# Key blocks of a two-mixer decoder layer: second copies by DMA, and another bank for the eighth value tile

## The chip, the core and the metric

The kernel runs on one core of one Trainium2 chip. The metric is the device time of one execution in microseconds (us). TensorE (PE) multiplies into eight PSUM banks, VectorE (DVE), ScalarE (ACT) and GpSimd (POOL) work on vectors, and SyncE (SP) issues nearly all DMAs of this kernel.

## The reference, cut to what matters

One decoder layer over 1024 tokens of width 1024. A normalised and modulated input `h` is projected to queries, keys and values of two token mixers with two key heads each, to gates and to a merge. One mixer is a banded attention (window 128, `swa`); the other adds a compressed, a block-selected (`slc`) and a banded attention (window 512, `win`).

```python
h = rms_norm(x, g_pre[l]) * (1.0 + scale[:, None, :]) + shift[:, None, :]
proj = h @ w_in[l]
q_a, kv_c, kv_s, kv_w, g_nsa, z_a, q_b, kv_b, z_b, merge = jnp.split(proj, pts, axis=-1)
o_a = gts[0] * o_cmp + gts[1] * o_slc + gts[2] * o_win
o_b = banded_attention(qb, kv_heads(kb_, ...), kv_heads(vb_, ...), slopes_b, SWA_WINDOW, sinks=sinks[l])
y = (sigmoid(m_a) * y_a + sigmoid(m_b) * y_b) @ w_out[l]
x = x + gate[:, None, :] * rms_norm(y, g_post[l])
```

## The kernel before

**Numbers in two parts.** Every large product is three matmuls. A float32 operand is split into a high part in TensorE's rounded format and a low part that is the rest; high x high, low x high and high x low are added in one PSUM bank. A score needs two matmuls: the query tile holds the 64 high rows of a head on one half of the partitions and its 64 low rows on the other, and the key tile must therefore hold the same key rows on both halves. That is the second copy this case is about. `kh` is the high part of the keys, twice; `kl` the low part, twice.

**Key blocks.** `k_block` (L488) takes a bank with the projected keys of two key heads, 64 rows each, and for each head r: ACT copies the high part to half r of the partitions (L500), DVE subtracts for the low part (L508), DVE copies both to the other half (L510, L511). Where the tile is that of a banded mixer's second half of the tokens, it also holds the last 128 columns of the first half in front (L503, L504); a `slc` tile has 64 columns of compressed keys there (L506, L507). The second head's L500 waits for the first head's L508. There are six key blocks: `swa` in two halves, and `slc` with `win` in two halves for each of two groups, so 12 heads and 24 second copies, and 8 copies of a first block.

**Stages.** (1) A prologue to about 56 us forms the first half of `h` and, while it arrives, four value tiles in banks `s`, `s`, `s`, `pt` and the first key and query columns in `fb`: banks `pj`, `pj`, `pt`. (2) Two compression inputs are projected, the second half of `h` is formed, and the value tiles five to seven are multiplied together (72 matmuls, L210 to L212) in the three `s` banks, then tile eight alone (24 matmuls). `v_out` (L238) takes a value tile off its bank: a high part on ACT (L242), a low part on DVE (L243), the gate columns on DVE (L244). (3) Next the compression's second halves (L187 onwards), its MLP, and gate projections. (4) Four units, two of `swa` and two of the other mixer, from about 180 us to 680 us: scores (L770, L773), softmax, transposes (L841), split of the weights (L847 on ACT, L848 on DVE), weighted values (L849, L852) into the one `pv` bank, which ACT and DVE read at the task's end (L861, L862). Projections for later work fill TensorE between them (L900 to L905). (5) The two output projections and the merge.

**What sets the order.** PSUM banks come from four rings: three `s`, two `pt`, one `pv`, two `pj`. A bank is reused when the last reader of its earlier content is done. The code is scheduled by the Tile framework, which simulates a timeline and writes each engine's instructions in a fixed order; `chain` ties the order of some of them (tags `act`, `dve`, `kout`, `pj`, ...). Each engine then runs its own list in order and waits on semaphores. SP issues DMAs in its listed order too: a DMA whose input is not ready holds all that stand behind it. Weights come in halves of 256 KB (`wraw`, three buffers), are split by ACT or DVE and POOL into `wh` and `wl` (six buffers each). At the end of a task `zt` is loaded and `od` stored by SP; `ot` and `zt` have one buffer each.

Of the kernel before, what the change touches and what calls it, by code (L numbers as in the profile page):

```python
# [7 lines left out]
F32 = mybir.dt.float32  # L8
# [6 lines left out]
P = 128  # L15
D = 1024
S = 1024
HS = 512
# [50 lines left out]
def hybrid_kernel(tc, io, out):  # L69
    nc = tc.nc  # L70
# [9 lines left out]
    def bank(tag):  # L80
        return ps.tile([P, 512], F32, tag=tag, name=f"b_{tag}", bufs=BANKS[tag])
# [3 lines left out]
    def chain(tag, ins):  # L85

        if tag in last and last[tag].ins.engine == ins.ins.engine:
            tc.add_manual_dep(
                ins.ins, last[tag].ins.name,
                mybir.DependencyInfo(mybir.DependencyClass.NoSync, mybir.DependencyReason.DATA), reason=tag)  # L90
        last[tag] = ins
# [88 lines left out]
    def proj_half(w, half, get, between=None):  # L180
        t = get()
        for kc in range(KC):
            mid = between() if between and kc == 2 else None
            if mid:
                after(mid, ins)
            wh, wl = (x[:, kc % KH, :] for x in w[kc // KH])
            ins = nc.tensor.matmul(t, lhsT=wh, rhs=hh[kc][half], start=(kc == 0), stop=False)  # L187
            if mid:
                after(ins, mid)
            if kc == 0:  # L190
                chain("pj", ins)
                if hold[0] is not None:
                    after(ins, hold[0])
            nc.tensor.matmul(t, lhsT=wh, rhs=hl[kc][half], start=False, stop=False)  # L194
            nc.tensor.matmul(t, lhsT=wl, rhs=hh[kc][half], start=False, stop=(kc == KC - 1))  # L195
        return t
# [8 lines left out]
    def v_products(half, k, i, t, w):  # L205

        sl = slice(i * P, i * P + P)
        wh, wl = w
        return [
            lambda: nc.tensor.matmul(t[:, :408], lhsT=hh[k][half][:, sl], rhs=wh, start=(k == 0), stop=False),  # L210
            lambda: nc.tensor.matmul(t[:, :408], lhsT=hh[k][half][:, sl], rhs=wl, start=False, stop=False),
            lambda: nc.tensor.matmul(t[:, :408], lhsT=hl[k][half][:, sl], rhs=wh, start=False, stop=(k == KC - 1))]  # L212
# [8 lines left out]
    def in_turn(products, between=(), at=2):  # L221

        for n in range(3):
            if n == at:
                for f in between:
                    f()
            for fs in products:
                ins = fs[n]()
                if n == 0:
                    chain("kout", ins)  # L230

    def dve(ins):
        chain("dve", ins)
        return ins

    def act(ins):
        chain("act", ins)
        return ins  # L238

    def v_out(i, t):  # L240
        tv = t[:, :384].rearrange("p (h d) -> p h d", h=6)
        high = nc.scalar.copy(V[i][:, :, 0, :], tv)  # L242
        low = nc.vector.tensor_tensor(V[i][:, :, 1, :], tv, V[i][:, :, 0, :].bitcast(F32), ALU.subtract)  # L243
        rest = nc.vector.tensor_copy(gates[:, i].rearrange("p b g r -> p (b g r)"), t[:, 384:408])  # L244
        act(high)
        dve(low)
        dve(rest)
# [15 lines left out]
    with tc.tile_pool(name="pro", bufs=1, reuse_waits="tile") as pro:  # L263
# [61 lines left out]
        vb = [bank(b) for b in ("s", "s", "s", "pt")]  # L325
        fb = [bank(b) for b in ("pj", "pj", "pt")]
# [68 lines left out]
        for k in range(KC):  # L395
            nxt = loads(k + 1) if k + 1 < KC else None
            t = pro.tile([P, HS], F32, name="ht", tag="ht", bufs=3)
# [91 lines left out]
    def k_block(keys, half, w, t=None, act=lambda i: i, dve=lambda i: i):  # L489
        if t is None:  # L490
            t = proj_half(w, half, lambda: bank("pj"))
        for r in range(2):
            src = t[64 * r : 64 * r + 64, :]

            pre, tag, bufs = (P, "kts", 8) if keys[r][0] == "slc" or half else (0, "kt", 6)
            khp = kq.tile([P, pre + HS], F32R, name="kh", tag=tag, bufs=bufs)
            klp = kq.tile([P, pre + HS], F32R, name="kl", tag=tag, bufs=bufs)
            kh, kl = khp[:, pre:], klp[:, pre:]
            hi, lo = kh[64 * r : 64 * r + 64, :], kl[64 * r : 64 * r + 64, :]
            chain(tag, act(nc.scalar.copy(hi, src)))  # L500
            if pre and keys[r][0] != "slc":
                before = K[(keys[r], 0)]
                nc.vector.tensor_copy(khp[:, :P], before[0][:, HS - P :].bitcast(F32))  # L503
                nc.vector.tensor_copy(klp[:, :P], before[1][:, HS - P :].bitcast(F32))  # L504
            elif pre:
                nc.vector.tensor_copy(khp[:, pre - 64 : pre], kc2[:, 0, keys[r][1], :].bitcast(F32))  # L506
                nc.vector.tensor_copy(klp[:, pre - 64 : pre], kc2[:, 1, keys[r][1], :].bitcast(F32))  # L507
            dve(nc.vector.tensor_tensor(lo, src, hi.bitcast(F32), ALU.subtract))  # L508
            o0, o1 = 64 - 64 * r, 128 - 64 * r
            dve(nc.vector.tensor_copy(kh[o0:o1, :], hi.bitcast(F32)))  # L510
            dve(nc.vector.tensor_copy(kl[o0:o1, :], lo.bitcast(F32)))  # L511
            K[(keys[r], half)] = (khp, klp)

    def q_fills(mixer, g, half):
# [2 lines left out]
    def k_fills(mixer, g, half):  # L517
        if mixer == "B":
            return [lambda: k_block([("swa", 0), ("swa", 1)], half, load_block("KB"))]
        return [lambda: k_block([("slc", g), ("win", g)], half, load_block(f"KA{g}"))]  # L520
# [33 lines left out]
    vb = [bank("s") for _ in range(3)]  # L554
    for k in range(KC):
        in_turn([v_products(1, k, i, vb[i], vw_all[k]) for i in range(3)])
    v_out(4, vb[0])
    t = bank("s")
    for k in range(KC):
        in_turn([v_products(1, k, 3, t, vw_all[k])])  # L560
    k_block([("swa", 0), ("swa", 1)], 0, None, fb[0], act, dve)
    v_out(5, vb[1])
    v_out(6, vb[2])
    v_out(7, t)
# [691 lines left out]
```

## Time and profile before

| | |
|---|---|
| median of 3 runs | 908.1 us (908.0 to 910.78) |
| profiled execution: its time | 909.31 us |
| its span, first to last instruction | 907.5 us |
| granted TensorE clock | 0.998 |
| PE busy, weight loads busy | 894.1 us (99%), 755.8 us (83%) |
| DVE, ACT, POOL busy | 554.3, 505.3, 352.8 us |
| share of DMA engines on the SP queue | 32.9% |

A row of the timeline gives the start in us, the time that the merged instructions took, engine, line, operation, tiles (output<-inputs, numbers left out), shapes and how many; in brackets the idle time of the engine before it, with what ended it. Consecutive matmuls overlap: the time of one (0.39 us for 512 columns) is longer than the distance to the next start (0.23 us), so distances are taken from start to start.

### The profile page before, as it was taken

The page shows a single profiled execution, that of the slowest core. Times are in us where ns is not written, and L with a number is a line of the kernel's source. Part 1 is how long each engine was busy: PE and PEld are TensorE (multiplying, and loading weights), DVE is VectorE, ACT ScalarE, POOL GpSimd, SP SyncE. Part 2 cuts the span into 40 slices and gives each one's busy share as a digit, 9 for nine tenths or more (in the row PEclk, how much of TensorE's full clock was granted, in tenths as well). Part 3 has the DMA queues.
Part 4 walks back from the last instruction along what each step waited for, and adds up shares of the span by engine and source line. Part 5 has one row for each costly group of instructions (what it writes and reads, how often), then busy time and mean ns, then how long its engine had stood idle before and what let it go on. Part 6 is the DMA issues. An engine that isn't in the chain of part 4 may idle for free.

```text
span 907.5 us, 14317 instructions
## 1 busy us (share of the span) xinstructions
PE 894.1 (99%) x4568; PEld 755.8 (83%) x4568; DVE 554.3 (61%) x1546; ACT 505.3 (56%) x1151; POOL 352.8 (39%) x422
## 2 busy tenths in 40 slices
PE   9999999999999999999999999999999999999997
PEld 8889888888888878888888878888887888887885
DVE  5866864475577787675576687566464372677322
ACT  5476732476676767665656667565564564441111
POOL 0000411364675866443545566453442375200000
PEclk9999999999999999999999999999999999999999
DMA  8872442333233312111211211111202587334422
GB/s 313 299 262 69 140 159 85 117 94 105 83 105 101 98 51 69 59 44 64 70 47 60 70 55 63 59 47 60 81 30 77 204 259 228 104 113 184 137 95 88
DMA packets 63870, 100.84 MB, mean 111 GB/s; under 512 B 7473, under 2 KB 24241, under 8 KB 63794
## 3 DMA queue, kind: packets, MB, share of 16 engines
q1 hardware_dynamic: 62640, 98.69, 32.9%
q10 hardware_dynamic: 1154, 1.23, 0.4%
q8 instruction: 36, 0.59, 0.3%
q14 instruction: 40, 0.33, 0.1%
HBM read 79.97 MB, written 19.92 MB: 110 GB/s over the span
## 4 chain that ended last, share of the span: by engine, by line
PE 94%; DVE 3%; ACT 1%; issue 1%; DMA 0%; POOL 0%; DVEq 0%; POOLq 0%; ACTq 0%
PE b_pt L841 8%; PE b_pj L900 7%; PE b_pj L904 7%; PE b_pj L905 7%; PE b_pj L194 5%; PE b_pj L195 5%; PE b_pj L187 5%; PE b_s L773 4%; PE b_s L770 4%; PE b_pv L852 4%; PE b_pv L849 4%; PE b_s L1140 1%; PE b_s L1139 1%; PE b_s L1141 1%; PE b_pt L294 1%; PE b_s L210 1%
## 5 line engine op out<-in xcount | busy, mean ns | idle before, releaser
L164 POOL TENSOR_TENSOR wl<-wraw,wh 128x512 fp32r<-128x512 f32 x102 | 132.8, 1305 | 140.2 <-ACT wh L161 91.9
L848 DVE TENSOR_TENSOR pl<-b_pt,ph 128x512 fp32r<-128x512 f32 x162 | 110.3, 686 | 55.5 <-ACT ph L847 54.6
L847 ACT CAST ph<-b_pt 128x512 fp32r<-128x512 f32 x162 | 93.5, 584 | 63.5 <-PE b_pt L841 52.7
L900 PE MATMUL b_pj<-hh,wh 128*128 128x512 f32 x288 | 117.1, 410 | 0.0
L905 PE MATMUL b_pj<-hh,wl 128*128 128x512 f32 x288 | 113.8, 395 | 0.0
L904 PE MATMUL b_pj<-hl,wh 128*128 128x512 f32 x288 | 113.3, 395 | 0.0
L195 PE MATMUL b_pj<-hh,wl 128*128 128x512 f32 x240 | 94.6, 394 | 0.0
L187 PE MATMUL b_pj<-hh,wh 128*128 128x512 f32 x240 | 94.5, 394 | 0.0
L194 PE MATMUL b_pj<-hl,wh 128*128 128x512 f32 x240 | 94.2, 392 | 0.0
L804 POOL TENSOR_SCALAR ps<-ps,rr,gates 128x128 f32<-128x128 f32 (+7 forms) x64 | 52.5, 822 | 94.6 <-DVE rr L796 50.0
L770 PE MATMUL b_s<-kh,q 128*128 128x256 f32 (+6 forms) x272 | 85.8, 322 | 0.0
L792 ACT ACTIVATE ps<-ps,mins 128x256 f32<-128x256 f32 (+7 forms) x96 | 64.9, 678 | 36.6 <-DVE mins L780 32.3
L773 PE MATMUL b_s<-kl,q 128*128 128x256 f32 (+6 forms) x272 | 83.8, 316 | 0.0
L161 ACT CAST wh<-wraw 128x512 fp32r<-128x512 f32 x94 | 57.8, 617 | 39.2 <-PE b_pj L194 13.6
L792 ACT ACTIVATE pw<-pw,mins 128x256 f32<-128x256 f32 (+4 forms) x96 | 60.7, 634 | 23.9 <-DVE mins L780 23.6
L849 PE MATMUL b_pv<-ph,V 128*128 128x512 f32 x162 | 65.5, 404 | 3.5 <-DVE ot L862 3.5
L852 PE MATMUL b_pv<-pl,V 128*128 128x512 f32 x162 | 67.9, 419 | 0.3
L905 PEld LDWEIGHTS b_pj<-hh,wl 128*128 128x128 f32 x288 | 54.1, 188 | 10.8
L863 POOL TENSOR_TENSOR ot<-ot,zt 64x512 f32<-64x512 f32 x32 | 41.7, 1303 | 55.0 <-DVE ot L862 43.5
L904 PEld LDWEIGHTS b_pj<-hl,wh 128*128 128x128 f32 x288 | 54.3, 189 | 8.8
L900 PEld LDWEIGHTS b_pj<-hh,wh 128*128 128x128 f32 x288 | 53.8, 189 | 7.8
L804 POOL TENSOR_SCALAR pw<-pw,rr,gates 128x640 f32<-128x640 f32 (+4 forms) x64 | 47.2, 741 | 31.7 <-DVE rr L796 28.6
(298 smaller groups left out, 2138.8 us busy)
## 6 DMA issues: line engine op xcount, KB each, us to landing
wraw<-in_w_blk SPq DMA_DIRECT2D x90, 256.0 KB, 2.9
wa<-in_w_adaT SPq DMA_DIRECT2D x24, 512.0 KB, 5.6
w1raw<-in_w SPq DMA_DIRECT2D x16, 256.0 KB, 3.2
od<-ot SPq DMA_DIRECT2D x64, 64.0 KB, 2.1
sp_MA<-sp SPq DMA_DIRECT2D x16, 256.0 KB, 2.0
wraw<-in_w_o SPq DMA_DIRECT2D x16, 256.0 KB, 3.0
wraw<-in_w_out SPq DMA_DIRECT2D x16, 256.0 KB, 3.4
t<-od SPq DMA_DIRECT2D x16, 256.0 KB, 3.9
```

The costliest lines, as they stand in the source:

```text
L164: chain("wl", nc.gpsimd.tensor_tensor(wl, raw, wh.bitcast(F32), ALU.subtract))
L187: ins = nc.tensor.matmul(t, lhsT=wh, rhs=hh[kc][half], start=(kc == 0), stop=False)
L194: nc.tensor.matmul(t, lhsT=wh, rhs=hl[kc][half], start=False, stop=False)
L195: nc.tensor.matmul(t, lhsT=wl, rhs=hh[kc][half], start=False, stop=(kc == KC - 1))
L770: ins = nc.tensor.matmul(sp[:, :n_in], lhsT=q, rhs=rh, start=True, stop=False)
L773: nc.tensor.matmul(sp[:, :n_in], lhsT=q, rhs=rl, start=False, stop=True)
L792: nc.scalar.activation(rows[r][:, :off], rows[r][:, :off], AF.Exp, scale=-1.0, bias=last_min[:, r : r + 1], accum_out=sums[:, r : r + 1])
L848: nc.vector.tensor_tensor(pl, t, ph.bitcast(F32), ALU.subtract)
L852: nc.tensor.matmul(pv, lhsT=v, rhs=pl, start=False, stop=(last and n == len(todo) - 1))
L900: ins = nc.tensor.matmul(self.t, lhsT=wh, rhs=hh[kc][self.half], start=(kc == 0), stop=False)
L904: nc.tensor.matmul(self.t, lhsT=wh, rhs=hl[kc][self.half], start=False, stop=False)
L905: ins = nc.tensor.matmul(self.t, lhsT=wl, rhs=hh[kc][self.half], start=False, stop=(kc == KC - 1))
```

## The change

In `k_block` the two copies of a first block (L503, L504) and the two second copies of each head (L510, L511) are no longer DVE instructions; each is a DMA from SBUF to SBUF on SP's queue. The 64 columns of compressed keys stay on DVE. In stage 2 the first key block is written ahead of the eighth value tile and ahead of the fifth tile's `v_out`, and the eighth tile's bank comes from the `pj` ring instead of the `s` ring.

```diff
@@ -500,15 +500,15 @@
             chain(tag, act(nc.scalar.copy(hi, src)))
             if pre and keys[r][0] != "slc":
                 before = K[(keys[r], 0)]
-                nc.vector.tensor_copy(khp[:, :P], before[0][:, HS - P :].bitcast(F32))
-                nc.vector.tensor_copy(klp[:, :P], before[1][:, HS - P :].bitcast(F32))
+                nc.sync.dma_start(khp[:, :P].bitcast(F32), before[0][:, HS - P :].bitcast(F32))
+                nc.sync.dma_start(klp[:, :P].bitcast(F32), before[1][:, HS - P :].bitcast(F32))
             elif pre:
                 nc.vector.tensor_copy(khp[:, pre - 64 : pre], kc2[:, 0, keys[r][1], :].bitcast(F32))
                 nc.vector.tensor_copy(klp[:, pre - 64 : pre], kc2[:, 1, keys[r][1], :].bitcast(F32))
             dve(nc.vector.tensor_tensor(lo, src, hi.bitcast(F32), ALU.subtract))
             o0, o1 = 64 - 64 * r, 128 - 64 * r
-            dve(nc.vector.tensor_copy(kh[o0:o1, :], hi.bitcast(F32)))
-            dve(nc.vector.tensor_copy(kl[o0:o1, :], lo.bitcast(F32)))
+            nc.sync.dma_start(kh[o0:o1, :].bitcast(F32), hi.bitcast(F32))
+            nc.sync.dma_start(kl[o0:o1, :].bitcast(F32), lo.bitcast(F32))
             K[(keys[r], half)] = (khp, klp)
 
     def q_fills(mixer, g, half):
@@ -554,11 +554,11 @@
     vb = [bank("s") for _ in range(3)]
     for k in range(KC):
         in_turn([v_products(1, k, i, vb[i], vw_all[k]) for i in range(3)])
-    v_out(4, vb[0])
-    t = bank("s")
+    k_block([("swa", 0), ("swa", 1)], 0, None, fb[0], act, dve)
+    t = bank("pj")
     for k in range(KC):
         in_turn([v_products(1, k, 3, t, vw_all[k])])
-    k_block([("swa", 0), ("swa", 1)], 0, None, fb[0], act, dve)
+    v_out(4, vb[0])
     v_out(5, vb[1])
     v_out(6, vb[2])
     v_out(7, t)
```

The order of the built programs shows three places. First DVE where the second half of `h` ends (L306) and the fifth to eighth value tiles are taken off; `b_pj_160` is the first keys' bank, `b_s_764` the fifth tile's. Before:

```order
L306 TENSOR_TENSOR hl7_117<-xh_640,hh7_101 128x512
L243 TENSOR_TENSOR V4_133<-b_s_764,V4_133 128x6x64
L244 COPY gates_85<-b_s_764 128x24
L508 TENSOR_TENSOR kl_868<-b_pj_160,kh_867 64x512
L510 CAST kh_867<-kh_867 64x512
L511 CAST kl_868<-kl_868 64x512
L508 TENSOR_TENSOR kl_874<-b_pj_160,kh_873 64x512
L510 CAST kh_873<-kh_873 64x512
L511 CAST kl_874<-kl_874 64x512
L243 TENSOR_TENSOR V5_134<-b_s_765,V5_134 128x6x64
```

And now, to the eighth tile in `b_pj_851`:

```order
L306 TENSOR_TENSOR hl7_117<-xh_640,hh7_101 128x512
L508 TENSOR_TENSOR kl_840<-b_pj_160,kh_839 64x512
L508 TENSOR_TENSOR kl_846<-b_pj_160,kh_845 64x512
L243 TENSOR_TENSOR V4_133<-b_s_764,V4_133 128x6x64
L244 COPY gates_85<-b_s_764 128x24
L243 TENSOR_TENSOR V5_134<-b_s_765,V5_134 128x6x64
L244 COPY gates_85<-b_s_765 128x24
L243 TENSOR_TENSOR V6_135<-b_s_766,V6_135 128x6x64
L244 COPY gates_85<-b_s_766 128x24
L634 MEMSET kcf_1092 128x128
L649 MEMSET vcf_1224 128x128
L243 TENSOR_TENSOR V7_136<-b_pj_851,V7_136 128x6x64
```

Both key subtractions moved ahead of the value tiles, and their four copies are gone. On PE the list is the same there but for the bank: the eighth tile's 24 matmuls are followed at once by the compression's projection into `b_pj_915` (L187), as before. In the built program the eighth tile's first matmul now waits for the second key subtraction (before: for the fifth tile's L244), and that L187 waits for the eighth tile's L244 (before: for the second key subtraction).

The second place is DVE in the third unit (and, with the same rows, in the fourth), where the keys of the second half of the tokens are made while a task ends. Before:

```order
L820 TENSOR_TENSOR pl_3765<-b_pt_3761,ph_3764 128x256
L503 CAST kh_3876<-kh_2987 128x128
L848 TENSOR_TENSOR pl_3829<-b_pt_3823,ph_3828 128x512
L508 TENSOR_TENSOR kl_3869<-b_pj_3754,kh_3868 64x512
L510 CAST kh_3868<-kh_3868 64x512
L511 CAST kl_3869<-kl_3869 64x512
L504 CAST kl_3877<-kl_2988 128x128
L506 CAST kh_5279<-kc2_137 128x64
L508 TENSOR_TENSOR kl_3877<-b_pj_3754,kh_3876 64x512
L510 CAST kh_3876<-kh_3876 64x512
L862 TENSOR_TENSOR ot_3775<-b_pv_3621,ot_3775 64x512
L511 CAST kl_3877<-kl_3877 64x512
```

Now:

```order
L820 TENSOR_TENSOR pl_3765<-b_pt_3761,ph_3764 128x256
L848 TENSOR_TENSOR pl_3829<-b_pt_3823,ph_3828 128x512
L508 TENSOR_TENSOR kl_3869<-b_pj_3754,kh_3868 64x512
L508 TENSOR_TENSOR kl_3877<-b_pj_3754,kh_3876 64x512
L506 CAST kh_5279<-kc2_137 128x64
L862 TENSOR_TENSOR ot_3775<-b_pv_3621,ot_3775 64x512
```

Six copies have left the list ahead of and around L862, which frees the `pv` bank. The third place is SP at the same point; now:

```order
L151 DMA wraw_4174<-in_w_blk 128x512
L503 DMA kh_3876<-kh_2987 128x128
L510 DMA kh_3868<-kh_3868 64x512
L511 DMA kl_3869<-kl_3869 64x512
L504 DMA kl_3877<-kl_2988 128x128
L510 DMA kh_3876<-kh_3876 64x512
L511 DMA kl_3877<-kl_3877 64x512
L151 DMA wraw_4315<-in_w_blk 128x512
L866 DMA od0_118<-ot_3775 64x2x128
L866 DMA od1_119<-ot_3775 64x2x128
```

Before, `wraw_4315` followed `wraw_4174` at once; the six key DMAs stand between them, and the stores of the task (`od`) come after. On all engines together the list differs in many small ways from about 95 us to 400 us and in the fourth unit around the key block, since the scheduler placed its fill-in work anew.

## The prediction

> **What bounds the kernel now.** I read the page's busy times and chain first, then the list of what PE waited for, then the timeline at each of those waits.
>
> ```profile
> PE 894.1 (99%) x4568; PEld 755.8 (83%) x4568; DVE 554.3 (61%) x1546; ACT 505.3 (56%) x1151; POOL 352.8 (39%) x422
> PE 94%; DVE 3%; ACT 1%; issue 1%; DMA 0%; POOL 0%; DVEq 0%; POOLq 0%; ACTq 0%
> PE b_pv L849 <- DVE ot L862: 3.5, 2, 1.8
> PE b_pt L294 <- DVE eps L309: 1.0, 1, 1.0
> PE b_s L210 <- DVE gates L244: 1.0, 1, 1.0
> PE b_pt L841 <- DVE pl L848: 0.6, 2, 0.3
> PE b_pt L614 <- ACT w L610: 0.3, 1, 0.3
> ```
>
> PE is busy for 99% of the span and holds 94% of the chain. The change takes no matmul away, so it can win only PE's waits. The list is all of them: 6.4 us, 1.0 of it (L294) at the very start. The other 5.4 us are five stops at three places that the change touches, and one (L614) just behind. DVE's total (61%) does not matter; only where it is late does.
>
> **First place: the eighth value tile.** The rows run from the last three matmuls of tiles five to seven to the first of tile eight.
>
> ```profile
> 75.59 0.82 ACT L303 ACTIVATE xh<-xh,mod 128x512 f32<-128x512 f32 x1
> 76.44 0.69 DVE L306 TENSOR_TENSOR hl<-xh,hh 128x512 fp32r<-128x512 f32 x1 [0.86 <-ACT xh L303]
> 79.18 0.72 PE L212 MATMUL b_s<-wvh,hl 128*128 128x408 f32 x3
> 79.94 0.58 ACT L500 CAST kh<-b_pj 64x512 fp32r<-64x512 f32 x1
> 80.56 0.17 DVE L244 COPY gates<-b_s 128x24 f32<-128x24 f32 x1
> 80.64 0.67 DVE L508 TENSOR_TENSOR kl<-b_pj,kh 64x512 fp32r<-64x512 f32 x1
> 80.87 0.42 PE L210 MATMUL b_s<-wvh,hh 128*128 128x408 f32 x1 [0.97 <-DVE gates L244]
> ```
>
> Matmuls of 408 columns start 0.186 us apart (24 of them from 80.87 to 85.39 are 0.188 each), so without a wait tile eight would begin at 79.18 + 3 x 0.186 = 79.74. It began at 80.87: **1.13 us lost**, from start to start. Now it waits for the two key subtractions instead. Their bank has been full since the prologue, and both stand right behind the last L306, which ends at 77.13. ACT is free at 76.41: L500 to 76.99, L508 from 77.13 to 77.80, second L500 to 78.41, second L508 to about 79.1. With the 0.14 us between L244's end (80.73) and PE's start that is 79.25, ahead of 79.74. The stop goes.
>
> It comes back behind the tile, because the projection that follows (L187) now takes the bank that tile eight leaves:
>
> ```profile
> 85.21 0.34 PE L212 MATMUL b_s<-wvh,hl 128*128 128x408 f32 x1
> 85.39 0.40 PE L187 MATMUL b_pj<-hh,wh 128*128 128x512 f32 x1
> 85.59 0.34 ACTq L630 DMA_DIRECT2D w2k<-in_w2k  x1
> 85.97 0.48 ACT L242 CAST V<-b_s 128x384 fp32r<-128x384 f32 x1 [3.15 <-PE b_s L212]
> 86.96 0.17 DVE L244 COPY gates<-b_s 128x24 f32<-128x24 f32 x1
> ```
>
> From the tile's last matmul (85.21) to the end of its L244 (87.13) are 1.92 us: the matmul's end, a DMA issue on ACT's queue, the high part, the low part, the gates. With 0.14 for the semaphore, L187 can start 2.06 us after that matmul, where 0.18 would do: **a new wait of 1.88 us**. Everything here stands 1.13 earlier, so L187 starts at 85.39 - 1.13 + 1.88 = 86.14. The first place loses **0.75 us** net. Queued behind that L187 are the compression and its MLP, all of PE's list; the queries (L485, L486) follow the eighth tile on ACT and DVE and are 1.13 us earlier than before, so the scores that need them do not stop PE again. The L614 stop (0.3 us) may go, since ACT's gate work moves ahead of it; I count 0 and leave it to the range.
>
> **Second and third place: the keys of the second half, in both long units.** From top to bottom POOL, DVE, ACT and PE of the third unit.
>
> ```profile
> 331.75 1.29 POOL L164 TENSOR_TENSOR wl<-wraw,wh 128x512 fp32r<-128x512 f32 x1
> 331.44 1.68 DVE L503 CAST kh<-kh 128x128 fp32r<-128x128 f32 x1
> 333.05 0.68 DVE L848 TENSOR_TENSOR pl<-b_pt,ph 128x512 fp32r<-128x512 f32 x1
> 333.65 0.67 DVE L508 TENSOR_TENSOR kl<-b_pj,kh 64x512 fp32r<-64x512 f32 x1
> 335.12 0.23 DVE L504 CAST kl<-kl 128x128 fp32r<-128x128 f32 x1
> 336.66 0.68 DVE L862 TENSOR_TENSOR ot<-b_pv,ot 64x512 f32<-64x512 f32 x1
> 334.35 0.58 ACT L500 CAST kh<-b_pj 64x512 fp32r<-64x512 f32 x1 [2.50 <-DVE kl L508]
> 334.96 0.59 ACT L861 COPY ot<-b_pv 64x512 f32<-64x512 f32 x1
> 333.30 0.36 PE L824 MATMUL b_pv<-pl,vc 128*128 128x256 f32 x1
> 335.00 0.60 PE L841 MATMUL b_pt<-ident,ps 128*128 128x128 f32 x4
> 337.39 0.50 PE L849 MATMUL b_pv<-ph,V 128*128 128x512 f32 x1 [1.80 <-DVE ot L862]
> 338.66 0.63 PE L841 MATMUL b_pt<-ident,pw 128*128 128x128 f32 x4 [0.30 <-DVE pl L848]
> ```
>
> The chain reads: a 128x128 cast that elsewhere takes 0.23 us (L504) takes 1.68 and ends with POOL's L164 (333.12 against 333.04); it delays the first L508, that the second L500, that ACT's L861, and with four casts of 0.23 to 0.42 us between them L862 frees `pv` at 337.34, while PE stood there at 335.43 (four transposes at 0.108). After the change: L848 takes the cast's slot at 331.44, L508 at 332.04 to 332.71, second L500 to 333.33, second L508 to 334.03, behind it L506, a cast of L504's kind (0.23). ACT's L861 waits for PE's last L824 (333.66) and ends at 334.3; L862 ends at 335.0, before PE comes. The split for the next transposes follows L862 (0.69, to 335.7), in time for L841 at 335.43 + 3 x 0.23 = 336.12. Before it was 338.66: **2.54 us gained**.
>
> ```profile
> 532.51 1.68 DVE L503 CAST kh<-kh 128x128 fp32r<-128x128 f32 x1
> 536.09 0.60 PE L841 MATMUL b_pt<-ident,ps 128*128 128x128 f32 x4
> 539.63 0.63 PE L841 MATMUL b_pt<-ident,pw 128*128 128x128 f32 x4 [0.30 <-DVE pl L848]
> ```
>
> The fourth unit repeats it: 539.63 - (536.09 + 0.43 + 0.69) = **2.42 us**. The lists of PE and ACT are unchanged at both stops.
>
> The row on POOL is where a page bears on it. The Trainium skill, SBUF — State Buffer, section "SBUF: two separate sides", calls the port pair of DVE and GpSimd "an exclusive lock": a DVE copy within SBUF waits out a running GpSimd instruction. The trace agrees, 333.12 against 333.04. By it the wait leaves with the cast, as L848 and L508 read PSUM; were the wait DVE's own, the first rival's time would follow.
>
> **The other copies, and the DMAs.** 24 second copies and 8 first blocks leave DVE. At the other four key blocks PE waits for nothing on DVE, so they are worth 0. In exchange SP issues 32 DMAs.
>
> ```profile
> L510 DVE CAST kh<-kh x12: 420/422/1451, 81.3 to 537.2; 64x512 fp32r<-64x512 f32 x12
> od<-ot SPq DMA_DIRECT2D x64, 64.0 KB, 2.1
> wa<-in_w_adaT SPq DMA_DIRECT2D x24, 512.0 KB, 5.6
> 190.74 1.01 SPq L151 DMA_DIRECT2D wraw<-in_w_blk  x2
> 196.92 1.25 SPq L866 DMA_DIRECT2D od<-ot  x2
> 199.97 0.36 PE L770 MATMUL b_s<-kh,q 128*128 128x256 f32 x1
> ```
>
> No row shows a DMA within SBUF. The nearest, `od` of 64 KB out of SBUF, lands after 2.1 us; the farthest, 512 KB loads, after 5.6. I take 2.1 and keep 5.6. An `od` issue holds SP for 0.63. The tightest consumer is the `swa` block at 190: in SP's order seven of its DMAs (the eighth goes out earlier) stand ahead of the weights issued at 190.74, so the last goes out by 190.74 + 7 x 0.63 = 195.2 and lands at 197.3 (200.8 at 5.6). By its place in PE's list the first score on these keys is the L770 at 199.97, and it reads the first of the two heads, whose last DMA is four earlier (192.7 + 2.1 = 194.8). Behind the seven wait weights that PE uses over 10 us later and the `od` pair of 196.92, still ahead of its time. Cost 0; at 5.6 us still 0.
>
> **Sum.** Span 907.5 + 0.75 - 2.54 - 2.42 = 903.3. The profiled execution took 909.31, 1.8 more than its span; with that 905.1, or 4.2 less than it was. The runs' median, 908.1, stands 1.2 below the profiled one, so the prediction is **903.9 us**. Its own range is 902.5 to 905.3: 0.5 less if L614's stop and small change go too, and up to 1.4 more if each `pv` stop keeps some 0.7 to another reader.
>
> **Rivals.** (a) The stretched cast's time moves to the next instruction on DVE. Then L848 starts at 333.05 still, L508 at 333.65, second L500 ends at 334.93, second L508 at 335.6, L506 at 335.85, L862 at 336.5; PE starts at 336.6 where 335.43 was asked. The stops shrink only by 0.8 each: 908.1 + 0.75 - 1.6 = 907.2. For it: L503's start stands before POOL's L164. Against it: L504 and L510 run in 0.23 and 0.42 us when POOL is idle. (b) The new wait behind tile eight is longer, because the query block's readers (L485, L486), not L244, free the bank that L187 gets. Two heads of it on ACT and DVE in turn, taken as the keys' L500 and L508, are 2 x (0.58 + 0.67) = 2.5 us more: 906.4. Against it the built program's wait, which names L244. (c) The scheduler's new order from 95 to 400 us has a stop of the old kind somewhere, where DVE or POOL is slower than planned: one of 2.4 us makes 906.3. For it: the two stops above came about so. Against it: seven of the eight units and halves ran without one. (d) Slower: the DMAs within SBUF are slow, and PE waits for keys. The price starts in the `swa` block at 190 us: issue of the first head's copies ends by 192.7, the score is at 199.97, so each us of landing beyond 7.3 is one us of PE. From 14.2 us on (7.3 + 4.2 + 2.7) the kernel is slower by 0.3%; at 15 it is 911.6. Against it every landing of 2.0 to 5.6 us on this queue. (e) More than forecast: POOL and DVE, freed of each other, win small stops elsewhere, below 902.5; the list of PE's waits leaves little for it.
>
> **Chances.** Forecast 0.53, (a) 0.10, (b) 0.07, (c) 0.16, (d) 0.08, (e) 0.06. A measurement of this kernel tells 0.3% (2.7 us) from no change, so faster means below 905.4. That holds the forecast, (e) and some of (c), where the stop is below 1.5 us: faster 0.65. Same takes (a), (b), the rest of (c) and a thin part of the forecast's edge: 0.27. Slower is (d): 0.08. The range that holds 8 in 10 reaches from 902.2 to 907.6, over (a) to (c).
>
> **What would show it.** After: the wait L210 <- L244 gone; a new wait of about 1.7 us of L187 on L244 near 84 us; no L849 <- L862 near 331 and 532; L503, L504, L510, L511 only as DMAs, landing in 2 to 3 us; PE never waiting on one. Wrong, if L849 still waits there over 0.5 us, if L187 starts later than 86.6, or if PE waits for a key DMA.

## The result, and the profile after

The changed kernel takes 904.35 us (median of 6 runs, 902.3 to 905.22) where the kernel before takes 908.09 (907.75 to 910.78): a ratio of 0.9950 with a 95% interval of 0.9939 to 0.9961. The forecast was 903.9, inside its range of 902.2 to 907.6, and faster by more than 0.3%.

The page of the changed kernel, busy times and the chain by engine:

```profile
PE 893.1 (99%) x4568; PEld 755.4 (84%) x4568; DVE 539.0 (60%) x1514; ACT 504.0 (56%) x1151; POOL 354.8 (39%) x422
PE 99%; DVE 0%; ACT 0%; issue 0%; DVEq 0%; POOLq 0%; ACTq 0%
```

DVE's 3% of the chain are gone and PE now holds 99% of it. The whole list of what PE waited for (us in total, times, longest):

```profile
PE b_pj L187 <- DVE gates L244: 1.7, 1, 1.7
PE b_pt L294 <- DVE eps L309: 1.0, 1, 1.0
PE b_s L770 <- DVE minc L786: 0.2, 1, 0.2
```

Both stops of L849 on L862 and both of L841 on L848 are gone, L210's stop on L244 has become L187's, the L614 stop is gone, and one small stop is new.

**First place.** The timeline of the changed kernel, from the last key subtraction to the projection behind the eighth tile:

```profile
78.19 0.69 DVE L508 TENSOR_TENSOR kl<-b_pj,kh 64x512 fp32r<-64x512 f32 x1 [0.65 <-ACT kh L500]
79.00 0.72 PE L212 MATMUL b_s<-wvh,hl 128*128 128x408 f32 x3
79.55 0.35 PE L210 MATMUL b_pj<-wvh,hh 128*128 128x408 f32 x1
...
83.85 0.34 PE L212 MATMUL b_pj<-wvh,hl 128*128 128x408 f32 x1
...
85.61 0.17 DVE L244 COPY gates<-b_pj 128x24 f32<-128x24 f32 x1
85.93 0.47 PE L187 MATMUL b_pj<-hh,wh 128*128 128x512 f32 x1 [1.74 <-DVE gates L244]
```

Tile eight starts 0.55 us after the group of three, without a stop. L187 starts 2.08 after the tile's last matmul, where 0.19 would do: 1.89 lost (forecast 1.88). It starts at 85.93; forecast was 86.14, in an execution whose first L210 stood 0.20 later (16.93 against 16.73).

**Second and third place.** The same stretch of the third unit as in the prediction, now the rows of DVE, POOL, ACT and PE that the argument needs, then two PE rows of the fourth unit:

```profile
332.41 0.67 DVE L848 TENSOR_TENSOR pl<-b_pt,ph 128x512 fp32r<-128x512 f32 x1
333.01 0.67 DVE L508 TENSOR_TENSOR kl<-b_pj,kh 64x512 fp32r<-64x512 f32 x1
334.33 0.69 DVE L508 TENSOR_TENSOR kl<-b_pj,kh 64x512 fp32r<-64x512 f32 x1 [0.65 <-ACT kh L500]
335.34 0.68 DVE L862 TENSOR_TENSOR ot<-b_pv,ot 64x512 f32<-64x512 f32 x1
332.72 1.28 POOL L164 TENSOR_TENSOR wl<-wraw,wh 128x512 fp32r<-128x512 f32 x1
334.72 0.58 ACT L861 COPY ot<-b_pv 64x512 f32<-64x512 f32 x1 [0.43 <-PE b_pv L824]
335.98 0.60 PE L841 MATMUL b_pt<-ident,ps 128*128 128x128 f32 x4
336.33 0.47 PE L849 MATMUL b_pv<-ph,V 128*128 128x512 f32 x1
337.10 0.60 PE L841 MATMUL b_pt<-ident,pw 128*128 128x128 f32 x4
534.07 0.60 PE L841 MATMUL b_pt<-ident,ps 128*128 128x128 f32 x4
535.20 0.60 PE L841 MATMUL b_pt<-ident,pw 128*128 128x128 f32 x4
```

L164 still runs on POOL, beside L848 and L508, and neither is longer than elsewhere (0.67). L862 ends at 336.02, ahead of L849 at 336.33. From one L841 to the next are 1.12 us where 3.66 were, and 1.13 where 3.54 were: 2.54 and 2.41 us gained.

**The DMAs.** All 32, with the size and the median time from issue to landing:

```profile
kh<-kh SPq DMA_DIRECT2D x12, 128.0 KB, 2.3
kl<-kl SPq DMA_DIRECT2D x12, 128.0 KB, 2.3
kh<-kh SPq DMA_DIRECT2D x4, 64.0 KB, 2.9
kl<-kl SPq DMA_DIRECT2D x4, 64.0 KB, 2.2
```

By these medians they land in 2.2 to 2.9 us (single ones in 1.9 to 3.7), near the 2.1 of `od` that the sum took, and no compute engine waits for one.

**Where 4.8 us of span went.** The table takes every matmul's distance to the next start less the median distance of its shape in the kernel before, adds these up over the program from the first L210 to the last matmul, and splits the sum by time, with the first L210 set to 16.8 us (a column also holds small losses that are no stop, and one of 0.08 can fall on either side of a column's edge).

| us that PE lost | 75-100 | 100-180 | 180-325 | 325-345 | 345-525 | 525-545 | rest | sum |
|---|---|---|---|---|---|---|---|---|
| before | 1.28 | 1.46 | 1.26 | 2.75 | 2.95 | 2.65 | 5.14 | 17.49 |
| after | 2.08 | 1.03 | 1.94 | 0.31 | 2.53 | 0.25 | 5.06 | 13.20 |
| e1 copies only | 1.31 | 1.59 | 1.25 | 0.22 | 2.50 | 0.25 | 5.87 | 12.99 |
| e2 move only | 2.06 | 0.85 | 1.39 | 2.73 | 2.95 | 2.68 | 5.16 | 17.82 |
| e3 first blocks by DMA | 1.28 | 1.34 | 1.34 | 1.20 | 2.99 | 0.97 | 5.16 | 14.28 |
| e4 second copies by DMA | 1.28 | 1.56 | 1.25 | 1.31 | 2.52 | 1.31 | 5.05 | 14.28 |
| e5 first blocks by maximum | 1.28 | 1.23 | 1.26 | 3.31 | 2.96 | 3.33 | 5.13 | 18.50 |
| e6 fifth tile first | 1.32 | 1.35 | 1.25 | 0.22 | 2.50 | 0.25 | 5.03 | 11.92 |
| e7 DMAs twice | 2.08 | 0.75 | 1.27 | 0.22 | 2.50 | 0.26 | 5.04 | 12.12 |
| e8 first blocks on ACT | 1.28 | 1.56 | 1.34 | 1.19 | 2.96 | 0.97 | 5.14 | 14.44 |
| e9 fifth tile first, tied | 0.07 | 1.21 | 1.26 | 0.25 | 2.49 | 0.25 | 4.99 | 10.52 |

After against before: +0.80 at the first place, -2.44 and -2.40 at the other two, -0.43 with the L614 stop (100-180), -0.42 in 345-525, +0.68 in 180-325, -0.08 elsewhere: -4.29. The start is 0.20 earlier and what follows the last matmul 0.29 shorter; together 4.8.

### The profile page after: what moved, and what is told of

Same layout as the page of the kernel before. It is cut to its first block, busy times and chain, and to the rows that moved or that the text cites. A ratio compares the mean times of both kernels' runs of the same rounds, so it can differ in the third digit from the quotient of the medians.

```text
span 902.7 us, 14354 instructions
## 1 busy us (share of the span) xinstructions
PE 893.1 (99%) x4568; PEld 755.4 (84%) x4568; DVE 539.0 (60%) x1514; ACT 504.0 (56%) x1151; POOL 354.8 (39%) x422
## 3 DMA queue, kind: packets, MB, share of 16 engines
q10 hardware_dynamic: 1154, 1.23, 0.5%
## 4 chain that ended last, share of the span: by engine, by line
PE 99%; DVE 0%; ACT 0%; issue 0%; DVEq 0%; POOLq 0%; ACTq 0%
PE b_pt L841 8%; PE b_pj L900 7%; PE b_pj L904 7%; PE b_pj L905 7%; PE b_pj L187 6%; PE b_pj L195 6%; PE b_pj L194 6%; PE b_s L773 5%; PE b_s L770 4%; PE b_pv L852 4%; PE b_pv L849 4%; PE b_s L1139 1%; PE b_s L1141 1%; PE b_s L1140 1%; PE b_pt L294 1%; PE b_s L1063 1%
## 5 line engine op out<-in xcount | busy, mean ns | idle before, releaser
L164 POOL TENSOR_TENSOR wl<-wraw,wh 128x512 fp32r<-128x512 f32 x102 | 135.2, 1326 | 141.0 <-ACT wh L161 87.9
L848 DVE TENSOR_TENSOR pl<-b_pt,ph 128x512 fp32r<-128x512 f32 x162 | 110.3, 687 | 65.3 <-ACT ph L847 64.5
L187 PE MATMUL b_pj<-hh,wh 128*128 128x512 f32 x240 | 94.6, 394 | 1.7 <-DVE gates L244 1.7
L804 POOL TENSOR_SCALAR ps<-ps,rr,gates 128x128 f32<-128x128 f32 (+7 forms) x64 | 52.4, 823 | 94.6 <-DVE rr L796 54.6
L770 PE MATMUL b_s<-kh,q 128*128 128x256 f32 (+6 forms) x272 | 85.4, 322 | 0.2 <-DVE minc L786 0.2
L849 PE MATMUL b_pv<-ph,V 128*128 128x512 f32 x162 | 65.7, 405 | 0.0
L804 POOL TENSOR_SCALAR pw<-pw,rr,gates 128x640 f32<-128x640 f32 (+4 forms) x64 | 47.3, 742 | 32.9 <-DVE rr L796 25.4
L841 PE MATMUL b_pt<-ident,ps 128*128 128x128 f32 x344 | 57.8, 272 | 0.0
```

Of the source, the lines that this page charges most:

```text
L164: chain("wl", nc.gpsimd.tensor_tensor(wl, raw, wh.bitcast(F32), ALU.subtract))
L770: ins = nc.tensor.matmul(sp[:, :n_in], lhsT=q, rhs=rh, start=True, stop=False)
L841: ins = nc.tensor.transpose(t[:, r * P : r * P + P], rows[r][:, off : off + P], ident)
L848: nc.vector.tensor_tensor(pl, t, ph.bitcast(F32), ALU.subtract)
```

## The experiments

The time from launch to the first L210 differs between executions of the same instructions: 16.73, 16.79 and 16.95 in three of the changed kernel, 17.37 and 16.44 in two of e9, 14.35 and 13.84 in e8 and e7, whose lists are the same up to there. Runs of one kernel spread by 2 to 6 us. So beside the medians stands the time from the first L210 to the last matmul of the profiled execution: 883.66 before, 879.37, 879.18 and 880.01 for the changed kernel.

**The copies alone (e1) and the move alone (e2).** e1 undoes the second part of the change, e2 does only that part.

```diff
@@ e1, against the changed kernel; e2 is the reverse, against the kernel before @@
-    k_block([("swa", 0), ("swa", 1)], 0, None, fb[0], act, dve)
-    t = bank("pj")
+    v_out(4, vb[0])
+    t = bank("s")
     for k in range(KC):
         in_turn([v_products(1, k, 3, t, vw_all[k])])
-    v_out(4, vb[0])
+    k_block([("swa", 0), ("swa", 1)], 0, None, fb[0], act, dve)
```

> All key copies by DMA, but the eighth value tile in its old bank and the first key block behind it, as in the kernel before. My theory (the copies bring all the gain, the move of the eighth tile costs about 0.75 us): both stops of L849 on L862 are gone, the stop of the eighth tile's first L210 on L244 is back (1.0 us in the list of waits) in place of the stop of L187 on L244 (1.7 us); span 902.0 us, median about 903.6, that is 0.7 below the changed kernel. Rival (the move is needed, because without it the key copies or the tiles collide again): slower than the changed kernel, 905 or more.

> The changed kernel once more beside the three others, to compare them on one chip: 904.35 us, span 902.7, one stop of L187 on L244 of 1.7 us.

> The eighth value tile's bank and the first key block's place as in the change, all key copies still on DVE. My theory: both stops of L849 on L862 stay (3.5 us in the list of waits), the stop of L210 on L244 is replaced by one of L187 on L244 of about 1.7 us; 0.75 us slower than before, span 908.2, about 908.9 where before is 908.1. Rival (the move brings part of the gain): 907 or below.

Measured on one chip: e1 903.63 us (0.9932, 0.9916 to 0.9948), the changed kernel again 904.22 (0.9935, 0.9919 to 0.9951), e2 909.36 beside 909.49 (0.9998, 0.9990 to 1.0007). The two largest of what PE waited for in e2:

```profile
PE b_pv L849 <- DVE ot L862: 3.5, 2, 1.8
PE b_pj L187 <- DVE gates L244: 1.7, 1, 1.7
```

All the gain is in the copies. In the table the move costs 0.78 at the first place (2.06 - 1.28), as forecast, but 0.61 comes back in 100-180: the L614 stop has left the list, because ACT's split of the compression weights (L610) comes earlier. Before, an L530 of 0.60 us stood ahead of it in ACT's order (L530 at 112.35, L610 at 112.97); in e2, as in the changed kernel, L610 starts at 111.69 and the L530 follows at 113.78. Net e2 loses 0.33, too little for its interval to tell from nothing. e1's list has the old stops back and one that no theory had:

```profile
PE b_s L210 <- DVE gates L244: 1.0, 1, 1.0
PE b_pt L1139 <- ACT ymh L1107: 0.5, 1, 0.5
PE b_pt L614 <- ACT w L610: 0.3, 1, 0.3
```

The L1139 stop (0.8 in "rest") stands in the last stage. It also appears, with 0.3, in one of three executions of the changed kernel, so it need not come from the edit; its cause was not looked for. Without it e1 would be about 0.9 ahead of the changed kernel: 0.77 at the first place and 0.69 in 180-325, less 0.56 in 100-180.

**Which copies (e3, e4).** Each does one of the two kinds by DMA, in the kernel before.

```diff
@@ e3, against the kernel before @@
-                nc.vector.tensor_copy(khp[:, :P], before[0][:, HS - P :].bitcast(F32))
-                nc.vector.tensor_copy(klp[:, :P], before[1][:, HS - P :].bitcast(F32))
+                nc.sync.dma_start(khp[:, :P].bitcast(F32), before[0][:, HS - P :].bitcast(F32))
+                nc.sync.dma_start(klp[:, :P].bitcast(F32), before[1][:, HS - P :].bitcast(F32))
@@ e4, against the kernel before @@
-            dve(nc.vector.tensor_copy(kh[o0:o1, :], hi.bitcast(F32)))
-            dve(nc.vector.tensor_copy(kl[o0:o1, :], lo.bitcast(F32)))
+            nc.sync.dma_start(kh[o0:o1, :].bitcast(F32), hi.bitcast(F32))
+            nc.sync.dma_start(kl[o0:o1, :].bitcast(F32), lo.bitcast(F32))
```

> The kernel before with only the two copies of a first block (L503, L504) by DMA; the second copies stay on DVE and so does the eighth tile's old place. The order of DVE around the two stops is otherwise the same. My theory (two parts of one chain: the cast stretched by POOL's L164, and four plain casts ahead of L862): without the stretched cast L848 starts at 331.44, L862 ends at about 335.8 instead of 337.34, and the split after it about 336.9, so L849 still stops about 0.5 and L841 about 0.3: 1.7 us gained at each of the two places, about 904.7. Rival 1 (the stretched cast is the whole cause): 2.5 each, 903.1. Rival 2 (the time of the stretched cast moves to the next DVE instruction): 907.5.

> The kernel before with only the second copies (L510, L511) by DMA; the first blocks (L503, L504) stay on DVE. My theory: L503 still takes 1.6 to 1.7 us where POOL's L164 runs, L848 starts at 333.05 as before, but L862 ends about 336.4, and L849 stops about 1.0 us; 1.5 us gained at each place, about 905.1. Rival 1 (the stretched cast is the whole cause): nothing gained, 908. Rival 2 (the count of casts is the whole cause): 903.1 and no stop.

Measured: e3 906.1 (0.9957, 0.9944 to 0.9971), e4 905.47 (0.9949, 0.9933 to 0.9965), both beside 909.06. At the two places e3 gains 1.55 and 1.68 (expected 1.7), e4 1.44 and 1.34 (expected 1.5). What PE waited for in e3 keeps both kinds of stop, small:

```profile
PE b_pt L841 <- DVE pl L848: 0.6, 2, 0.3
...
PE b_pv L849 <- DVE ot L862: 0.2, 1, 0.2
```

In e4's timeline the cast is as long as before and ends with POOL's L164; behind it the list of e4's waits, where L849 stops for 0.8 each time:

```profile
331.27 1.67 DVE L503 CAST kh<-kh 128x128 fp32r<-128x128 f32 x1
...
331.58 1.28 POOL L164 TENSOR_TENSOR wl<-wraw,wh 128x512 fp32r<-128x512 f32 x1
```

```profile
PE b_pv L849 <- DVE ot L862: 1.6, 2, 0.8
```

So neither the stretched cast nor the plain casts are the whole cause. Alone each part is worth 1.3 to 1.7, together 2.4 to 2.5: the parts overlap, since only what makes L862 later than PE's own arrival counts. e4 also shows with what the 0.42 of 345-525 goes: it is gone where the second copies are DMAs (2.49 to 2.53) and there where they are not (2.95 to 2.99). Most of it lies between 450 and 480 us, in single distances at most 0.1 us over their median, with no named wait. PE's order differs there too: e2, e3, e5 and e8 keep the order of the kernel before, e4 and e1 have another. Whether the order or the copies cost it stays open.

**Whose wait the stretched cast is (e5, e8).** Both leave the four second copies on DVE.

```diff
@@ e5, against the kernel before @@
-                nc.vector.tensor_copy(khp[:, :P], before[0][:, HS - P :].bitcast(F32))
-                nc.vector.tensor_copy(klp[:, :P], before[1][:, HS - P :].bitcast(F32))
+                for x, o in ((before[0], khp), (before[1], klp)):
+                    x = x[:, HS - P :].bitcast(F32)
+                    nc.vector.tensor_tensor(o[:, :P], x, x, ALU.max)
@@ e8, against the kernel before @@
-                nc.vector.tensor_copy(khp[:, :P], before[0][:, HS - P :].bitcast(F32))
-                nc.vector.tensor_copy(klp[:, :P], before[1][:, HS - P :].bitcast(F32))
+                nc.scalar.copy(khp[:, :P], before[0][:, HS - P :].bitcast(F32))
+                nc.scalar.copy(klp[:, :P], before[1][:, HS - P :].bitcast(F32))
```

> The kernel before with the two copies of a first block made on DVE still, but as a maximum of the block with itself (a two-operand instruction, same values) instead of a cast. My theory (a copy within SBUF waits for POOL, an instruction with two operands does not): the instruction at 331.44 takes about 0.3 us though POOL runs, L862 ends about 336.1, L849 stops 0.7 and L841 0.3: 1.5 us gained at each place, about 905.1. Rival (any DVE instruction that only touches SBUF waits for POOL, or the stretch has another cause): it takes 1.6 us again, 908 or more.

> The kernel before with the two copies of a first block (L503, L504) on ACT in place of DVE; nothing else is changed, and DVE's order around the two stops is that of e3_first_by_dma. My theory (DVE and POOL share a way into SBUF, ACT has its own): L503 takes about 0.3 us on ACT while POOL's L804 and L164 run, and the gain is that of e3_first_by_dma less the 0.3 us that ACT's L861 may come later: 1.2 to 1.6 us at each place. Rival (any copy from these tiles is slow while POOL runs): over 1 us on ACT too, and L500 and L861 behind it late by as much: nothing gained or slower.

e5 is slower: 910.38 beside 909.06 (1.0019, 1.0007 to 1.0031). My theory of e5 fell. Its timeline, DVE and POOL:

```profile
330.97 1.75 DVE L505 TENSOR_TENSOR kh<-kh 128x128 fp32r<-128x128 f32 x1
...
334.71 0.29 DVE L505 TENSOR_TENSOR kl<-kl 128x128 fp32r<-128x128 f32 x1
...
329.37 1.95 POOL L805 TENSOR_SCALAR pw<-pw,rr,gates 128x384 f32<-128x384 f32 x3
331.28 1.28 POOL L164 TENSOR_TENSOR wl<-wraw,wh 128x512 fp32r<-128x512 f32 x1
...
337.04 0.86 DVE L512 CAST kl<-kl 64x512 fp32r<-64x512 f32 x1
336.34 1.27 POOL L164 TENSOR_TENSOR wl<-wraw,wh 128x512 fp32r<-128x512 f32 x1 [3.77 <-ACT wh L161]
```

The instruction with two operands takes 0.29 us with POOL idle and 1.75 beside it, and ends 0.16 after L164. The last two rows show why e5 is even slower than before: another L164 now runs beside a plain second copy (L512 here), which stands between L862 and the next split (L848) and takes 0.86 and, in the fourth unit, 0.94 us where 0.42 is usual. That is 0.44 and 0.52 of the 0.56 and 0.68 that the two places lose more.

On ACT (e8, 903.84 beside 909.35; 0.9946, 0.9928 to 0.9965) the same copy runs at its own pace:

```profile
329.37 0.30 ACT L503 CAST kh<-kh 128x128 fp32r<-128x128 f32 x1
...
327.46 1.94 POOL L804 TENSOR_SCALAR pw<-pw,rr,gates 128x384 f32<-128x384 f32 x3
329.37 1.29 POOL L164 TENSOR_TENSOR wl<-wraw,wh 128x512 fp32r<-128x512 f32 x1
```

All eight of its copies take 0.298 to 0.302 us, four of them beside a POOL instruction, and the gains are 1.56 and 1.68, those of e3. From the first L210 to the last matmul e8 takes 880.62 and e3 880.46; the 2.6 us by which e8's profiled span is the shorter (901.9 against 904.5) lie in the start (14.35 against 16.98). So it is DVE that waits for POOL, where all its operands are in SBUF, while DVE's reads of PSUM go on beside POOL: of the 162 L848 of the changed kernel 97 overlap a POOL instruction, and they take 0.67 to 0.69 us as the other 65 do. The Trainium skill, SBUF — State Buffer, section "Who interferes with whom", says that a DVE instruction with two SBUF inputs contends with a GpSimd instruction that reads SBUF, and that a copy or cast can contend too, in a mode that uses two ports. e5 agrees with the first at 1.75 against 0.29, and e8 agrees with its sentence that ACT waits for no one; no run shows in which mode these casts run.

**The DMAs twice (e7).** Each of the 32 key DMAs is issued two times in a row, the same data to the same place.

```diff
@@ against the changed kernel; the same for L503, L504 @@
             nc.sync.dma_start(kh[o0:o1, :].bitcast(F32), hi.bitcast(F32))
             nc.sync.dma_start(kl[o0:o1, :].bitcast(F32), lo.bitcast(F32))
+            nc.sync.dma_start(kh[o0:o1, :].bitcast(F32), hi.bitcast(F32))
+            nc.sync.dma_start(kl[o0:o1, :].bitcast(F32), lo.bitcast(F32))
```

> The changed kernel with each of the 32 key DMAs issued twice in a row. My theory (SP and the landing have slack everywhere, so these DMAs cost nothing): PE waits for no key DMA and for no weight, the same as the changed kernel within 1 us: 904.4. Rival (the DMAs cost something that the gain hides, on SP's queue or by the weights behind them): as much again on top, 906 or more, with a wait of PE, ACT or DVE for a DMA.

Measured 903.45 beside 909.06 (0.9927, 0.9913 to 0.9942), not slower than the changed kernel. PE waits for no key DMA, and the landing is unchanged:

```profile
kh<-kh SPq DMA_DIRECT2D x24, 128.0 KB, 2.3
```

Its first 3 us of advantage in the profile (first L210 at 13.84) are the start's; behind it, it is 878.29, and in 180-325 it has 1.27 where the changed kernel has 1.94 to 2.04: PE's order of the fill-in work differs from 208 to 316 us. So the 32 cost PE nothing that can be measured. Off PE's path there is more waiting in e7: ACT waits 7.7 us for `od` stores at L861 (2.0 in the changed kernel), and POOL at L863 5.3 us for `zt` and, by the trace, once 0.9 for a key DMA (none in the changed kernel). Whether the doubled DMAs or the other order bring it was not separated.

**Taking both stops away (e6, e9).** The eighth tile's stop needs the fifth tile's bank earlier. The first two of the three tiles wait for the third only because the 72 matmuls go round the banks; e6 does the last two of the eight steps tile after tile, with the copies by DMA and the eighth tile in its old bank as in e1.

```diff
@@ e6, against e1 @@
-    for k in range(KC):
+    for k in range(KC - 2):
         in_turn([v_products(1, k, i, vb[i], vw_all[k]) for i in range(3)])
+    for i in range(3):
+        for k in range(KC - 2, KC):
+            in_turn([v_products(1, k, i, vb[i], vw_all[k])])
@@ e9, against e6 @@
-            in_turn([v_products(1, k, i, vb[i], vw_all[k])])
+            in_turn([v_products(1, k, i, vb[i], vw_all[k])], every=True)
...
-                if n == 0:
+                if n == 0 or every:
                     chain("kout", ins)
```

> All key copies by DMA, the eighth tile in its old bank, and of the three tiles that are multiplied together the last two of eight steps are done tile after tile, so that the fifth tile's bank is full 1.85 us earlier. My theory: the fifth tile's last L212 starts at 77.3 instead of 79.18, its L244 ends about 79.0, ahead of the eighth tile's first matmul at 79.74; neither L210 nor L187 stops, so 1.75 us less than the changed kernel: span 901.0, median about 902.6. Rival (the last low part of h, ready at 77.1, is late for the fifth tile, or the second key subtraction for L187): a new stop of 0.5 to 1.5 us at one of them, 903 to 904.

> As e6_fifth_first, but with every matmul of the last two steps tied to the written order, since there the scheduler had put the last L212 of the three tiles side by side again. My theory: the fifth tile's last L212 stands 1.85 us before the third tile's, its L244 ends before the eighth tile's first L210, so the stop of 1.13 us on L244 is gone and none takes its place at L187; 1.1 us less than e6_fifth_first from the first L210 to the last matmul (878.1), that is 877.0, and about 2 less than the changed kernel. Rival: PE is then earlier at L614 (113 us), where it waited 0.3 us for ACT's split of the compression weights, and stops there for 1.1 us more: nothing gained.

e6 (902.3 beside 909.49; 0.9925, 0.9910 to 0.9940) did not take the stop away, though its median met the expected 902.6; that agreement is luck. Only the first matmul of each step is tied to the written order, and the scheduler put the last L212 of the three tiles together again:

```profile
79.65 0.72 PE L212 MATMUL b_s<-wvh,hl 128*128 128x408 f32 x3
...
81.34 0.43 PE L210 MATMUL b_s<-wvh,hh 128*128 128x408 f32 x1 [0.97 <-DVE gates L244]
```

The stop is the old 1.14. With every matmul tied (e9) the fifth tile's last L212 stands at 77.76, and its L244 ends before the eighth tile starts:

```profile
77.76 0.34 PE L212 MATMUL b_s<-wvh,hl 128*128 128x408 f32 x1
...
79.13 0.17 DVE L244 COPY gates<-b_s 128x24 f32<-128x24 f32 x1
...
80.17 0.35 PE L210 MATMUL b_s<-wvh,hh 128*128 128x408 f32 x1
```

What PE waited for in e9 is the start and 0.2 at L614 (L617 there):

```profile
PE b_pt L294 <- DVE eps L309: 1.0, 1, 1.0
PE b_pt L617 <- ACT w L613: 0.2, 1, 0.2
```

From the first L210 to the last matmul it takes 876.70 (expected 877.0), the rival with the longer L614 stop is out, and the median is 902.12 beside 909.35 (0.9918, 0.9901 to 0.9935). Once more, beside the changed kernel:

> The kernel of e9_fifth_first_tied once more, now on one chip with the changed kernel: from the first L210 to the last matmul 876.7 against 879.2 to 879.4, so about 2.5 us faster. The time until the first L210 differs from execution to execution by more than that (13.8 to 17.4 us so far), so the medians should differ by 1.5 to 3.5.

> The changed kernel beside e9_beside_after: 879.2 to 879.4 us from the first L210 to the last matmul, median 903.5 to 904.5.

e9 902.33, the changed kernel 904.09, before 908.16 on the same chip: 0.9932 (0.9917 to 0.9947) against 0.9947 (0.9928 to 0.9967). The medians differ by 1.8 and the intervals overlap; in the profiled executions it is 876.69 against 880.01, of which about 0.6 is that execution's L1139 stop. By medians e9 (902.12 and 902.33) is level with e6 (902.3) and 1.8 us ahead of the changed kernel. By the time from the first L210 it is the fastest here: 876.7 against 878.1 in e6 and 879.2 to 879.4 in the changed kernel.

## Why the prediction was right

- **The bound and the list of PE's waits:** right. Everything that the change won or lost beyond 1 us is a stop that stood in that list or the one named as new.
- **First place, net 0.75 lost:** measured 0.80, and 0.78 in e2. The new stop was 1.89 for 1.88. That the move pays for nothing by itself is shown by e1.
- **Second and third place, 2.54 and 2.42 gained:** 2.54 and 2.41 from start to start. The chain behind them is shown by parts: e4 keeps the stretched cast and gives back 1.0 to 1.1 of the gain, e3 keeps the plain casts and gives back 0.7 to 0.9.
- **Rival (a), the stretched time moves to the next instruction:** the wait left with the cast, as L848 at 0.67 beside L164 shows. Rival (a) is out (only in e3 a later cast, the first L510 of each place, took 0.58 where 0.42 is usual); its price was also wrong. I took only L849's 0.8 and forgot that the split behind L862 (0.3) and the next L841 come earlier too: with its own times L841 would start at 336.6 + 0.69 = 337.3, a gain of 1.4 for each place, which is e4's 1.34 to 1.44, and so 906.1 and not 907.2.
- **The L614 stop, counted at 0:** mis-sized by 0.35 to 0.66. It went since ACT came earlier, as the prediction thought possible, but not by gate work moving ahead: an L530 moved behind the split. Counted from the first L210, PE arrived 0.64 earlier and the split 1.08 earlier.
- **Rival (c), a new stop from the scheduler's order:** it happened in small. L770 at 306 us waits for L786 (0.2 in the list, 0.38 from start to start), and the stretch of 180 to 325 us lost 0.68 to 0.78; the rest of that has no named wait. Its price of 2.4 was three times too much. The argument against it miscounted: with two stops in eight units and halves, six ran without one, not seven.
- **The DMAs at 0:** right for PE, at 2.2 to 2.9 us of landing, and also twice over. Rivals (b) and (d) are out: L187 waited for L244, as the built order says, and nobody for a key.
- **Sum:** 903.9 forecast, 904.35 measured. In the profiled span 903.3 forecast and 902.7 measured; 0.5 of the surplus is the start and the tail, which no term covers. Three stretches counted at 0 moved by -0.43, -0.42 and +0.68 and cancel but for 0.17; that part of the agreement is luck.

## What to carry to other kernels

On a kernel whose TensorE is busy for 99%, list its waits first and price a change only at those: 20 of the 32 copies that left DVE stood at no stop, and the other 12 gave 4.8 us. A new bank for a tile moves a stop to whoever takes that bank next; ask for that reader before moving, and look whether the old bank can't be emptied earlier instead (here by finishing the first of three interleaved tiles ahead of the others, worth 1.25 us of e6's 1.32). Where a cast between SBUF tiles is several times its usual length, look for POOL beside it: here ACT did the same copy in 0.30 us and a DMA landed it in 1.9 to 3.3, while a two-operand DVE instruction waited as long as the cast.

## What the runs showed of the hardware

A cast that already waits can be passed over. In the kernel before, L503 was issued at 331.44, while the last of three L804 ran on POOL (to 331.79); the next POOL instruction, L164, went ahead of it at 331.75, and the cast ended only at 333.12, 0.08 after that. The fourth unit shows the same (532.51 to 534.19), and so do e4 and e5. It is no rule. The cast before it was stretched too, but it ended at 331.19, 0.05 after the second L804 (331.14), though the third had started at 331.12:

```profile
330.69 0.50 DVE L507 CAST kl<-kc 128x64 fp32r<-128x64 f32 x1
```

In e5 the stretched second copies likewise ended while POOL's next instruction ran. What decides it is open. Of the 40 copies of the key blocks on DVE in the kernel before, four took over 1.1 us; all four ended 0.08 to 0.28 us after a POOL instruction that ran beside them. The longer of the other two is in the `swa` block:

```profile
190.03 1.29 POOL L164 TENSOR_TENSOR wl<-wraw,wh 128x512 fp32r<-128x512 f32 x1 [0.73 <-ACT wh L161]
190.15 1.45 DVE L510 CAST kh<-kh 64x512 fp32r<-64x512 f32 x1
```

The start is the other surprise: the first L210 came between 13.84 and 17.37 us with PE's list the same up to there, in e7 after a wait for ACT's first high part:

```profile
13.84 0.46 PE L210 MATMUL b_s<-wvh,hh 128*128 128x408 f32 x1 [0.29 <-ACT hh L302]
```

That is more than most edits here are worth, so a comparison of one execution of each starts at that matmul. What decides it was not tried.
